# Forgetting attention: the key's forget sums and the causal mask added on VectorE instead of TensorE

## The chip, the cores and the metric

One core of a Trainium2 chip runs the whole program. The metric is the device time of one execution in microseconds, lower is better; the median of three runs of the kernel before is 2260.61 us (2258.91 to 2261.26).

## The reference, cut to what matters

Two layers on 512 tokens of width 2048. The second layer has three attention branches. Branch B, the one that is changed, is attention with forget gates: a running sum of log-gates per head is added to the scores.

```python
def forgetting_attention(q, k, v, f_logit, q_gain, k_gain):
    ...
    log_f = jax.nn.log_sigmoid(f_logit.astype(jnp.float32))
    c = jnp.cumsum(log_f, axis=1).transpose(0, 2, 1)
    ...
    def block_fn(args):
        qb, cqb, n = args
        sc = jnp.einsum('bqhd,bshd->bhqs', qb, k) * scale + cqb[..., None] - c[:, :, None, :]
        qpos = n * BLOCK + jnp.arange(BLOCK)
        mask = key_pos[None, :] <= qpos[:, None]
        sc = jnp.where(mask[None, None], sc, NEG)
        p = jax.nn.softmax(sc, axis=-1)
        return jnp.einsum('bhqs,bshd->bqhd', p, v)
```

B has 12 heads of 64 channels, 512 queries and 512 keys. The softmax of a row is the same without the query's own sum, which is one number for the whole row.

## The kernel before, in words

All matrix products use float32r operands. A float32 operand is split into a high part (a cast on ACT) and the rest (a subtraction on DVE), and a product becomes two or three products of parts. For weights, `Stream._piece` (L68) makes `whi` on ACT (L91) and `wlo` on DVE (L92) of each half of a tile that was loaded; it works two halves ahead of the products.

The program is written in the order in which the engines run it: each engine takes its instructions in program order. The main line is a sequence of projections (`proj`, L1236, or `logits`, L1288) into the PSUM banks `m0` to `m3`. Beside it, generators are advanced piece by piece: after each bank of a projection `step()` (L241) adds the generator's rate to a credit, and each full credit runs it to its next `yield`. The attention of a unit runs that way beside the projections of the next unit, at rate 0.41, one piece in about 2.4 steps, and what is left is run out by `drain()` ahead of the last tile of the second projection. There are six such units: one of kind C, two of A, three of B with four heads each. The three of B are called unit 0, 1 and 2 here; unit 2 runs beside the logits, whose results pass through `g` on DVE and ACT (L1295, L1296).

`attend` (L953) first normalizes and transposes queries and keys, whose splits go to `qk12` (L892 to L896). Then it goes through items. An item of B is a head and one of three sets of query blocks: blocks 0 and 1 with 128 and 256 keys, block 2 with 384, block 3 with 512. For each item there are these steps, of which two items are in flight:

- `s0` (L1049): score products into bank `s0` or `s1`, in turn; then on DVE the row maxima `nm` (L1084), and on ACT the exponentials into `pt`, with the sums of a row (L1089). In B each segment has two products `qk12` x key parts, one product that adds the key's sums (`cs`, a row selector scaled per head, times `mov`, the stored sums, L1067) and one that adds the mask to the diagonal block (`idr` x `dmr`, L1068). `cs` is made for the next head by ACT from `ct2` (L973, tile `cst`).
- `s2` (L1098), an iteration later: PE transposes the item's blocks of `pt` into the one bank `s2` (L1111), ACT casts them to `pth` (L1136) and DVE makes the rest, `ptl` (L1138), run by run.
- `s4` (L1140), when a head's last item is through: the products with the values into bank `s3`; `release` (L1019) then brings them to `os` (ACT L1029, DVE L1030), `finish` (L1032) divides by the row sums and gates with z (`un`), and `flush` (L1164) transposes that and writes `ur`.

`forget` (L907) makes the sums once, before the first unit: `mov` holds them for the products' moving side and `ct2` for the stationary side.

Kind A goes through the same steps. In its `s0` one DVE instruction adds a bias to the scores while it copies them to `pt` (L1080), and the maximum is taken from `pt` (L1082).

Of the kernel before, what the change touches and what calls it, by code (L numbers as in the profile page):

```python
# [14 lines left out]
P = 128  # L15
# [115 lines left out]
def _build(es, tc, nc, x, vecs, bgate, fg, sinks, bforget, w_mod, w_pin, w_grp, w_pout, mem, w_in, w_kv,  # L131
# [685 lines left out]
    idr = a3.tile([P, P], F32R, name="idr")  # L817
    S.copy(idr, idf)
    dmf = a3.tile([P, P], F32, name="dmf")
    nc.sync.dma_start(dmf, dmask)  # L820
    dmr = a3.tile([P, P], F32R, name="dmr")
    S.copy(dmr, dmf)
    rels = a3.tile([P, 256], F32, name="rels")
    nc.sync.dma_start(rels, rel)
    csl = a3.tile([P, 12], F32, name="csl")
    nc.sync.dma_start(csl, csel)
# [78 lines left out]
    ct2 = a3.tile([P, T], F32R, name="ct2")  # L905

    def forget(qk):  # L907
# [20 lines left out]
        for q in (32, 64, 96):  # L928
            V.tensor_copy(lf[:, :, q : q + 12], lf[:, :, 0:12])
# [7 lines left out]
        V.memset(r32(mov), 1.0)  # L937
        V.memset(r32(ct2), 1.0)
        S.copy(mov[0:64, :], b[0:64, :])
        V.tensor_tensor(out=mov[32:64, :], in0=b[32:64, :], in1=r32(mov[32:64, :]), op=sub)  # L940
        S.copy(ct2[64:128, :], b[64:128, :])
        V.tensor_tensor(out=ct2[96:128, :], in0=b[96:128, :], in1=r32(ct2[96:128, :]), op=sub)
# [10 lines left out]
    def attend(kind, unit, qk, vz):  # L953
# [12 lines left out]
        def head_state(h):  # L966
            if h not in hs:
                s = {}
                s["nm"] = a3.tile([P, NT], F32, tag="nm", name="nm", bufs=3)
                s["den"] = a3.tile([P, NT], F32, tag="den", name="den", bufs=3)  # L970
                if kind == "B" and "cs" not in s:
                    s["cs"] = a3.tile([P, T], F32R, tag="cst", name="cst", bufs=2)
                    S.activation(s["cs"], r32(ct2), AF.Copy, scale=csl[:, h0 + h : h0 + h + 1])  # L973
                hs[h] = s
            return hs[h]

        head_state(0)

# [70 lines left out]
        def s0(e):  # L1049
# [7 lines left out]
            for qt, c0, n in segs:  # L1057
                qs, bb = slice(qt * P, (qt + 1) * P), b[:, c0 : c0 + n]
                k0 = max(qt - 1, 0) * P if kind == "A" else 0
                ks = slice(k0, k0 + n)  # L1060
                if kind == "C":
                    mm3(bb, qkh[:, h, qs], qkl[:, h, qs], kch[:, h, ks], kcl[:, h, ks], True, True)
                else:
                    mm(bb, qk12[:, h, qs], kh[:, ks], start=True)
                    mm(bb, qk12[:, h, qs], kl[:, ks], stop=kind != "B")
                if kind == "B":
                    mm(bb, s["cs"][:, qs], mov[:, :n])  # L1067
                    mm(b[:, c0 + n - P : c0 + n], idr, dmr, stop=True)  # L1068
            if segs[0][0] == 0 and h + 1 < nh:
                head_state(h + 1)  # L1070
            pt = a3.tile([P, 512], F32, tag="pt", name="pt", bufs=2)
# [4 lines left out]
            for qt, m, c0, n in groups:  # L1076
                v = b[:, c0 : c0 + m * n].rearrange("p (m n) -> p m n", n=n)
                if kind == "A":
                    w = pt[:, c0 : c0 + m * n].rearrange("p (m n) -> p m n", n=n)
                    V.scalar_tensor_tensor(out=w, in0=rels[:, 256 - n :].unsqueeze(1).to_broadcast([P, m, n]), scalar=SLOPES[h0 + h],  # L1080
                                           in1=v, op0=mult, op1=add)
                    V.tensor_reduce(out=s["nm"][:, qt : qt + m], in_=w, axis=AX.X, op=vmax)  # L1082
                else:
                    V.tensor_reduce(out=s["nm"][:, qt : qt + m], in_=v, axis=AX.X, op=vmax, negate=True)  # L1084
# [3 lines left out]
            for qt, c0, n in segs:  # L1088
                S.activation(pt[:, c0 : c0 + n], (pt if kind == "A" else b)[:, c0 : c0 + n], AF.Exp, bias=s["nm"][:, qt : qt + 1],  # L1089
# [84 lines left out]

        ne = len(items)
        for e in range(ne + 2):
# [10 lines left out]
            if 1 <= e <= ne:  # L1187
                s2(e - 1)
            yield
# [177 lines left out]
def host_arrays(inputs):  # L1367
# [12 lines left out]
    for h in range(12):  # L1380
        csel[[h, 32 + h], h] = -1.0
        csel[[64 + h, 96 + h], h] = 1.0
# [31 lines left out]
```

## Time and profile before

| | |
|---|---|
| median of three runs | 2260.61 us |
| the profiled execution, its own time | 2261.89 us |
| its span, first to last instruction | 2260.1 us |
| mean granted TensorE clock | 0.993 of full speed |
| PE busy (matmuls) | 2212.2 us, 98% of the span |
| DVE busy | 1146.1 us, 51% |
| ACT busy | 883.1 us, 39% |
| attention of B, units 0, 1, 2 | begins about 1157, 1270 and 1385 us and lasts 60 to 70 us each |

PE is TensorE's matmuls, DVE VectorE, ACT ScalarE. Products go through the helper `mm` and so have the line L258 in every view. A row of the timeline gives an instruction's start and duration, its engine and line, and in square brackets how long the engine sat idle before it and what it then waited for last. Matmuls overlap in the pipeline, so what a product costs PE is the distance from its start to the next one's start, its pitch, and not its duration.

### The profile page before, as it was taken

Reading aid. Unit: us, or ns where it says so; the run is one execution under the profiler, and the core shown is the slowest. Engines: PE = TensorE matmul, PEld = TensorE weight load, DVE = VectorE, ACT = ScalarE, POOL = GpSimd, SP = SyncE. Lnnn points to the kernel's source line nnn. Section 1 sums busy time; section 2 is a strip of 40 time slices with the busy share of each in tenths; the row PEclk is TensorE's granted clock in tenths of the full one; section 3 lists DMA queues with packets and bytes.
Section 4 is the critical chain, followed back from the end, with each engine's and each line's share of the span. In section 5 each row is a group of like instructions: output and inputs, shape, how many; then the busy total and the mean of one; then the engine's idle time right before and its main releaser. Section 6 shows DMA issues by size and latency. Waiting matters only on the chain.

```text
span 2260.1 us, 26827 instructions
## 1 busy us (share of the span) xinstructions
PE 2212.2 (98%) x10199; PEld 1822.2 (81%) x10199; DVE 1146.1 (51%) x1996; ACT 883.1 (39%) x1719; POOL 0.2 (0%) x4
## 2 busy tenths in 40 slices
PE   7999999999999999999999999999999999999999
PEld 4678888888888988777778787788888888888887
DVE  3676655346665453756564655554334235336332
ACT  4433364333334353545464646542232222224221
POOL 0000000000000000000000000000000000000000
PEclk9989999999999999999999999999999999999999
DMA  9856633336664332222222222233333333333443
GB/s 329 280 165 208 202 103 98 98 121 225 223 224 128 97 83 75 75 75 75 75 75 75 75 75 75 66 100 96 94 93 102 97 99 94 102 94 98 154 131 112
DMA packets 164665, 275.12 MB, mean 122 GB/s; under 512 B 11074, under 2 KB 62776, under 8 KB 164280
## 3 DMA queue, kind: packets, MB, share of 16 engines
q1 hardware_dynamic: 164536, 273.41, 39.7%
q8 instruction: 80, 1.31, 0.2%
q14 instruction: 49, 0.40, 0.1%
HBM read 264.98 MB, written 8.39 MB: 121 GB/s over the span
## 4 chain that ended last, share of the span: by engine, by line
PE 82%; DVE 8%; ACT 5%; DMA 3%; issue 2%; SPq 0%; DVEq 0%; ACTq 0%
PE m L258 53%; PE s L258 26%; DVE wlo L92 2%; DVE qk L896 1%; DMA raw<-w_kv 1%; ACT pt L1089 1%; PE s L1111 1%; ACT whi L91 1%; DMA raw<-w_pout 1%; DVE acc L452 1%; ACT qk L892 1%; DVE nm L1082 1%; DVE pt L1080 1%; DVE ptl L1138 0%; DVE qk L862 0%
## 5 line engine op out<-in xcount | busy, mean ns | idle before, releaser
L92 DVE TENSOR_TENSOR wlo<-raw,whi 128x512 fp32r<-128x512 f32 (+2 forms) x740 | 493.7, 676 | 765.5 <-ACT whi L91 752.8
L91 ACT CAST whi<-raw 128x512 fp32r<-128x512 f32 (+2 forms) x740 | 441.3, 608 | 874.8 <-PE m L258 390.1
L258 PE MATMUL m<-whi,h_h 128*128 128x512 f32 (+2 forms) x960 | 373.8, 389 | 1.3 <-ACT whi L91 1.3
L258 PE MATMUL m<-wlo,h_h 128*128 128x512 f32 (+2 forms) x960 | 363.6, 379 | 2.9 <-DVE wlo L92 2.6
L258 PE MATMUL m<-whi,h_l 128*128 128x512 f32 (+2 forms) x960 | 363.1, 378 | 0.0
L258 PE MATMUL m<-h_h,whi 128*128 128x512 f32 x768 | 305.0, 397 | 0.0
L258 PE MATMUL m<-h_h,wlo 128*128 128x512 f32 x768 | 302.4, 394 | 1.0 <-DVE wlo L92 1.0
L258 PE MATMUL m<-h_l,whi 128*128 128x512 f32 x768 | 302.0, 393 | 0.0
L258 PEld LDWEIGHTS m<-wlo,h_h 128*128 128x128 f32 x960 | 181.5, 189 | 31.9 <-DVE wlo L92 6.1
L258 PEld LDWEIGHTS m<-whi,h_l 128*128 128x128 f32 x960 | 180.8, 188 | 31.5
L258 PEld LDWEIGHTS m<-whi,h_h 128*128 128x128 f32 x960 | 181.5, 189 | 27.6 <-ACT whi L91 1.6
L258 PE MATMUL s<-h_h,whi 128*128 128x512 f32 x512 | 200.8, 392 | 0.0
L258 PE MATMUL s<-h_l,whi 128*128 128x512 f32 x512 | 200.5, 392 | 0.0
L258 PE MATMUL s<-h_h,wlo 128*128 128x512 f32 x512 | 200.2, 391 | 0.0
L258 PEld LDWEIGHTS m<-h_h,wlo 128*128 128x128 f32 x768 | 145.7, 190 | 32.6 <-DVE wlo L92 1.5
L258 PEld LDWEIGHTS m<-h_h,whi 128*128 128x128 f32 x768 | 145.9, 190 | 30.4 <-ACT whi L91 0.8
L258 PEld LDWEIGHTS m<-h_l,whi 128*128 128x128 f32 x768 | 145.8, 190 | 29.6
L258 PEld LDWEIGHTS s<-h_h,wlo 128*128 128x128 f32 x512 | 96.8, 189 | 20.2
L258 PEld LDWEIGHTS s<-h_h,whi 128*128 128x128 f32 x512 | 96.8, 189 | 20.1
L258 PEld LDWEIGHTS s<-h_l,whi 128*128 128x128 f32 x512 | 96.9, 189 | 20.1
L258 PE MATMUL m<-whi,y_h 128*128 128x512 f32 x256 | 102.8, 402 | 1.4 <-DVE t L778 1.4
L258 PE MATMUL m<-whi,y_l 128*128 128x512 f32 x256 | 100.0, 391 | 0.0
(239 smaller groups left out, 2744.3 us busy)
## 6 DMA issues: line engine op xcount, KB each, us to landing
raw<-w_mod SPq DMA_DIRECT2D x96, 512.0 KB, 4.4
raw<-w_in SPq DMA_DIRECT2D x96, 512.0 KB, 3.8
raw<-w_pin SPq DMA_DIRECT2D x58, 512.0 KB, 3.8
raw<-w_in SPq DMA_DIRECT2D x96, 256.0 KB, 3.0
raw<-w_pout SPq DMA_DIRECT2D x32, 512.0 KB, 4.5
raw<-w_out SPq DMA_DIRECT2D x32, 512.0 KB, 3.7
raw<-w_in SPq DMA_DIRECT2D x32, 384.0 KB, 3.4
raw<-w_kv SPq DMA_DIRECT2D x16, 512.0 KB, 7.1
```

The costliest lines, as they stand in the source:

```text
L91: self.nc.scalar.copy(h3, v)
L92: self.nc.vector.tensor_tensor(out=l3, in0=v, in1=h3.bitcast(F32), op=ALU.subtract)
L258: PE.matmul(ps, lhsT=lhsT, rhs=rhs, start=start, stop=stop)
L452: V.scalar_tensor_tensor(out=acc, in0=v[:, e, :], scalar=w, in1=acc, op0=mult, op1=add)
L892: S.activation(hi[r, :], b[r, :], AF.Copy, scale=gain[r, :])
L896: V.scalar_tensor_tensor(out=outs[e][1][w, :], in0=b[r, :], scalar=gain[r, :], in1=r32(hi[r, :]), op0=mult, op1=sub)
L1080: V.scalar_tensor_tensor(out=w, in0=rels[:, 256 - n :].unsqueeze(1).to_broadcast([P, m, n]), scalar=SLOPES[h0 + h], in1=v, op0=mult, op1=add)
L1082: V.tensor_reduce(out=s["nm"][:, qt : qt + m], in_=w, axis=AX.X, op=vmax)
L1089: S.activation(pt[:, c0 : c0 + n], (pt if kind == "A" else b)[:, c0 : c0 + n], AF.Exp, bias=s["nm"][:, qt : qt + 1], accum_out=s["den"][:, ...
L1111: PE.transpose(b[:, x * P : (x + 1) * P], pt[:, c : c + P], idf)
```

## The change

In B's items the two products that add sums and mask are gone. PE leaves the scores in the bank; DVE adds the head's key sums while it moves them to `pt`, adds the mask to the diagonal block in `pt`, and takes the maximum from `pt`, as ACT takes the exponentials. The sums must now lie in every row, as `sums[h]` (tile `cst`, 128 x 512). `key_sums` makes them: one PE product of a selector `sel` with `mov` into bank `s3` and a copy by ACT. For a unit's first head it stands in a piece of its own ahead of the items, in bank `s0`; for the next head in the third item's iteration, behind `s2`. The selector (`pick`, 128 x 128) is made by ACT where `cs` was made. The queries' own sums are no longer added. The casts `idr` and `dmr`, `ct2`, two copies and a memset in `forget` are gone, and the rows of `csel` that served `ct2`.

```diff
-    idr = a3.tile([P, P], F32R, name="idr")
-    S.copy(idr, idf)
...
-    dmr = a3.tile([P, P], F32R, name="dmr")
-    S.copy(dmr, dmf)
...
-        for q in (32, 64, 96):
+        for q in (32,):
             V.tensor_copy(lf[:, :, q : q + 12], lf[:, :, 0:12])
...
-        V.memset(r32(mov), 1.0)
-        V.memset(r32(ct2), 1.0)
+        V.memset(r32(mov), 0.0)
         S.copy(mov[0:64, :], b[0:64, :])
         V.tensor_tensor(out=mov[32:64, :], in0=b[32:64, :], in1=r32(mov[32:64, :]), op=sub)
-        S.copy(ct2[64:128, :], b[64:128, :])
-        V.tensor_tensor(out=ct2[96:128, :], in0=b[96:128, :], in1=r32(ct2[96:128, :]), op=sub)
...
-                if kind == "B" and "cs" not in s:
-                    s["cs"] = a3.tile([P, T], F32R, tag="cst", name="cst", bufs=2)
-                    S.activation(s["cs"], r32(ct2), AF.Copy, scale=csl[:, h0 + h : h0 + h + 1])
...
+        def pick(h):
+            sel[h] = a3.tile([P, P], F32R, tag="sel", name="sel", bufs=2)
+            S.activation(sel[h], ones, AF.Copy, scale=ckl[:, h0 + h : h0 + h + 1])
+
+        def key_sums(h, tag="s3"):
+            b = bank(tag)
+            mm(b, sel.pop(h), mov, start=True, stop=True)
+            sums[h] = a3.tile([P, T], F32, tag="cst", name="cst", bufs=2)
+            S.copy(sums[h], b)
...
-                    mm(bb, qk12[:, h, qs], kl[:, ks], stop=kind != "B")
-                if kind == "B":
-                    mm(bb, s["cs"][:, qs], mov[:, :n])
-                    mm(b[:, c0 + n - P : c0 + n], idr, dmr, stop=True)
+                    mm(bb, qk12[:, h, qs], kl[:, ks], stop=True)
             if segs[0][0] == 0 and h + 1 < nh:
                 head_state(h + 1)
+                if kind == "B":
+                    pick(h + 1)
...
+                elif kind == "B":
+                    w = pt[:, c0 : c0 + m * n]
+                    V.tensor_tensor(out=w, in0=b[:, c0 : c0 + m * n], in1=sums[h][:, :n], op=add)
+                    dg = pt[:, c0 + n - P : c0 + n]
+                    V.tensor_tensor(out=dg, in0=dg, in1=dmf, op=add)
+                    V.tensor_reduce(out=s["nm"][:, qt : qt + m], in_=w, axis=AX.X, op=vmax, negate=True)
...
-                S.activation(pt[:, c0 : c0 + n], (pt if kind == "A" else b)[:, c0 : c0 + n], AF.Exp, bias=s["nm"][:, qt : qt + 1],
+                S.activation(pt[:, c0 : c0 + n], (b if kind == "C" else pt)[:, c0 : c0 + n], AF.Exp, bias=s["nm"][:, qt : qt + 1],
...
+        if kind == "B":
+            key_sums(0, "s0")
+            yield
         ne = len(items)
...
                 s2(e - 1)
+            if kind == "B" and e < ne and items[e][1][-1][0] == NT - 1 and items[e][0] + 1 < nh:
+                key_sums(items[e][0] + 1)
             yield
```

How the instructions stand now, at three places. The first is PE in unit 0 of B, the first item of the third head, before (`mov,cst` and `dmr,idr` are the products that go):

```order
L258 MATMUL s_9767<-qk_5578 128x128 x2
L258 MATMUL s_9767<-mov,cst 128x128
L258 MATMUL s_9767<-dmr,idr 128x128
L258 MATMUL s_9767<-qk_5578 128x256 x2
L258 MATMUL s_9767<-mov,cst 128x256
L258 MATMUL s_9767<-dmr,idr 128x128
L258 MATMUL m_9737<-whi,h_h_576 128x512
```

The same item on PE now, from the products of the projection ahead of it to those behind:

```order
L258 MATMUL m_9723<-whi,h_l_592 128x512
L258 MATMUL s_9785<-qk_5574 128x128 x2
L258 MATMUL s_9785<-qk_5574 128x256 x2
L258 MATMUL m_9724<-whi,h_h_576 128x512
L258 MATMUL m_9724<-wlo,h_h_576 128x512
```

Four products left this item, two each left the second and third. The second place is DVE from the third item of the second head to the first item of the third, in unit 0, before:

```order
L1030 TENSOR_TENSOR os<-s_9692,os 64x512
L1084 TENSOR_REDUCE nm<-s_9725 128x1
L1039 RECIPROCAL den<-den 128x4
L1043 TENSOR_TENSOR un<-vz,den 128x4x64
L92 TENSOR_TENSOR wlo<-raw,whi 128x512
L1138 TENSOR_TENSOR ptl<-s_9751,pth 128x128 x3
L1084 TENSOR_REDUCE nm<-s_9767 128x1 x2
```

And the same stretch of DVE now (`cst` holds the sums, `dmf` the mask):

```order
L1036 TENSOR_TENSOR os<-s_9701,os 64x512
L1090 TENSOR_TENSOR pt<-s_9738,cst 128x512
L1092 TENSOR_TENSOR pt<-pt,dmf 128x128
L1093 TENSOR_REDUCE nm<-pt 128x1
L1045 RECIPROCAL den<-den 128x4
L1049 TENSOR_TENSOR un<-vz,den 128x4x64
L1149 TENSOR_TENSOR ptl<-s_9755,pth 128x128 x3
L92 TENSOR_TENSOR wlo<-raw,whi 128x512
L1090 TENSOR_TENSOR pt<-s_9785,cst 128x128
```

Two adds stand ahead of each maximum, in the same place between the `ptl` of two items. The split `wlo` moved behind the `ptl`, since a piece more runs before the items and so each item meets the projection a few steps later; between a unit's first maximum or add and its last `ptl` there are 15 splits before and 15 now. The third place is the start of unit 0 on DVE, the last splits of queries and keys (`cols`) and the first item, before:

```order
L896 SCALAR_TENSOR_TENSOR qk_5578<-s_9465,cols,qk_5578 64x512 x2
L92 TENSOR_TENSOR wlo<-raw,whi 128x512
L896 SCALAR_TENSOR_TENSOR qk_5578<-s_9465,cols,qk_5578 64x512 x2
L1084 TENSOR_REDUCE nm<-s_9500 128x1 x2
L92 TENSOR_TENSOR wlo<-raw,whi 128x512
```

And now:

```order
L92 TENSOR_TENSOR wlo<-raw,whi 128x512
L892 SCALAR_TENSOR_TENSOR qk_5574<-s_9455,cols,qk_5574 64x512 x2
L92 TENSOR_TENSOR wlo<-raw,whi 128x512
L1090 TENSOR_TENSOR pt<-s_9507,cst 128x128
L1092 TENSOR_TENSOR pt<-pt,dmf 128x128
```

One weight split more stands ahead of the unit's first add. Unit 2 starts in the same way; in unit 1 a split stood there before, too.

## Rows read from the trace of the kernel before

**Rows 1.** The page's fourth part: shares of the chain of work that ended last, by engine.
```profile
PE 82%; DVE 8%; ACT 5%; DMA 3%; issue 2%; SPq 0%; DVEq 0%; ACTq 0%
```
**Rows 2.** Busy time by stretch, one row for each unit of B, from its first maximum to its last transposes: length, then busy us and instructions of PE, PE's weight loads, DVE, ACT and POOL, the granted TensorE clock, the DMA engines' share and GB/s.
```profile
1162.50:1220.00 57.50, 55.98 (x291) 46.84 (x290) 31.45 (x74) 30.60 (x85) 0.00 (x0) 1.00 0.24 70
1276.50:1335.50 59.00, 57.77 (x290) 48.41 (x291) 31.60 (x74) 30.72 (x85) 0.00 (x0) 0.97 0.24 72
1390.50:1452.50 62.00, 58.94 (x291) 47.97 (x291) 32.74 (x76) 37.04 (x91) 0.00 (x0) 0.97 0.22 65
```
**Rows 3.** Timeline of DVE, then of ACT, over a first item of a head in unit 1 (start us, duration us).
```profile
1304.08 0.61 DVE L1084 TENSOR_REDUCE nm<-s 128x1 f32<-128x128 f32 x2
1306.27 0.69 DVE L92 TENSOR_TENSOR wlo<-raw,whi 128x512 fp32r<-128x512 f32 x1 [1.57 <-ACT whi L91]
...
1308.74 0.69 DVE L92 TENSOR_TENSOR wlo<-raw,whi 128x512 fp32r<-128x512 f32 x1
1309.35 0.55 DVE L1084 TENSOR_REDUCE nm<-s 128x1 f32<-128x384 f32 x1
...
1303.74 0.73 ACT L973 ACTIVATE cst<-ct,csl 128x512 fp32r<-128x512 f32 x1
1304.81 0.37 ACT L1089 ACTIVATE pt<-s,nm 128x128 f32<-128x128 f32 x1 [0.34 <-DVE nm L1084]
...
1305.61 0.62 ACT L91 CAST whi<-raw 128x512 fp32r<-128x512 f32 x1
...
1309.99 0.58 ACT L1089 ACTIVATE pt<-s,nm 128x384 f32<-128x384 f32 x1 [1.28 <-DVE nm L1084]
```
**Rows 4.** Who waited for whom: us in total, times, longest us. First ACT, DVE and PE in the stretch of unit 0 (1162.5 to 1220), then ACT and DVE in that of unit 1 (1276.5 to 1335.5), then ACT in that of unit 2 (1390.5 to 1452.5).
```profile
ACT pt L1089 <- DVE nm L1084: 13.3, 11, 2.0
...
ACT pth L1136 <- PE s L1111: 4.0, 5, 1.8
...
DVE wlo L92 <- ACT whi L91: 10.6, 12, 2.8
...
PE s L1111 <- ACT pt L1089: 1.4, 1, 1.4
...
ACT pth L1136 <- PE s L1111: 3.9, 5, 1.7
...
DVE nm L1084 <- PE s L258: 0.5, 2, 0.4
...
ACT pth L1136 <- PE s L1111: 3.6, 4, 1.9
```
**Rows 5.** Timeline of unit 0: its first maxima, and the first cast of its last item.
```profile
1162.55 0.62 DVE L1084 TENSOR_REDUCE nm<-s 128x1 f32<-128x128 f32 x2
...
1219.63 0.27 ACT L1136 CAST pth<-s 128x128 fp32r<-128x128 f32 x1 [1.84 <-PE s L1111]
```
**Rows 6.** Timeline of PE: score products of a first item of B and the second and third product of the projection behind it; those of a second item of B and the second product behind it; those of a first item of A with the second product behind it (`m` is the projection's bank).
```profile
1302.46 0.34 PE L258 MATMUL s<-qk 128*128 128x128 f32 x2
...
1303.61 0.39 PE L258 MATMUL m<-wlo,h_h 128*128 128x512 f32 x1
1303.84 0.40 PE L258 MATMUL m<-whi,h_l 128*128 128x512 f32 x1
...
1307.28 0.51 PE L258 MATMUL s<-qk 128*128 128x384 f32 x2
...
1308.15 0.39 PE L258 MATMUL m<-wlo,h_h 128*128 128x512 f32 x1
...
956.11 0.62 PE L258 MATMUL s<-qk 128*128 128x128 f32 x4
...
956.79 0.40 PE L258 MATMUL m<-wlo,h_h 128*128 128x512 f32 x1
```
**Rows 7.** Timeline of DVE in two items of kind A, where an add (L1080) and a maximum (L1082) that needs it follow each other.
```profile
928.52 0.29 DVE L1080 SCALAR_TENSOR_TENSOR pt<-rels,s 128x128 f32<-128x128 f32 x1 [0.36 <-PE s L258]
928.84 0.29 DVE L1082 TENSOR_REDUCE nm<-pt 128x1 f32<-128x128 f32 x1
929.04 0.41 DVE L1080 SCALAR_TENSOR_TENSOR pt<-rels,s 128x256 f32<-128x256 f32 x1
929.49 0.42 DVE L1082 TENSOR_REDUCE nm<-pt 128x1 f32<-128x256 f32 x1
...
932.95 0.68 DVE L1080 SCALAR_TENSOR_TENSOR pt<-rels,s 128x512 f32<-128x512 f32 x1
933.66 0.69 DVE L1082 TENSOR_REDUCE nm<-pt 128x2 f32<-128x512 f32 x1
```
**Rows 8.** The group of ACT's copies out of bank `s3` over the whole span (busy us, mean ns; then idle time before them), and ACT's and DVE's timeline behind the last `pth` of a third item's step in unit 1.
```profile
L1029 ACT COPY os<-s 64x512 f32<-64x512 f32 x24 | 13.9, 581 | 9.7 <-PE s L258 9.2
...
1317.11 0.62 ACT L91 CAST whi<-raw 128x512 fp32r<-128x512 f32 x1
...
1317.77 0.69 DVE L92 TENSOR_TENSOR wlo<-raw,whi 128x512 fp32r<-128x512 f32 x1 [0.23 <-ACT whi L91]
```
**Rows 9.** Timeline of PE at the first transposes of unit 1, and two products of the projection behind them.
```profile
1279.05 1.14 PE L1111 MATMUL s<-idf,pt 128*128 128x128 f32 x3 [1.04 <-ACT pt L1089]
...
1280.85 0.63 PE L258 MATMUL m<-whi,h_l 128*128 128x512 f32 x1
1281.27 0.63 PE L258 MATMUL m<-whi,h_h 128*128 128x512 f32 x1
```

More of the change, by code (lines that the diff above doesn't have):

```diff
@@ L816, in _build @@
     a3 = p3.enter_context(tc.tile_pool(name="a3", bufs=1))
-    idr = a3.tile([P, P], F32R, name="idr")
-    S.copy(idr, idf)
     dmf = a3.tile([P, P], F32, name="dmf")
     nc.sync.dma_start(dmf, dmask)
-    dmr = a3.tile([P, P], F32R, name="dmr")
-    S.copy(dmr, dmf)
     rels = a3.tile([P, 256], F32, name="rels")
     nc.sync.dma_start(rels, rel)
-    csl = a3.tile([P, 12], F32, name="csl")
-    nc.sync.dma_start(csl, csel)
+    ckl = a3.tile([P, 12], F32, name="ckl")
+    nc.sync.dma_start(ckl, csel)
     snk = a3.tile([P, 12], F32, name="snk")
@@ L904, in _build @@
     mov = a3.tile([P, T], F32R, name="mov")
-    ct2 = a3.tile([P, T], F32R, name="ct2")
     def forget(qk):
@@ L970, in head_state @@
                 s["den"] = a3.tile([P, NT], F32, tag="den", name="den", bufs=3)
-                if kind == "B" and "cs" not in s:
-                    s["cs"] = a3.tile([P, T], F32R, tag="cst", name="cst", bufs=2)
-                    S.activation(s["cs"], r32(ct2), AF.Copy, scale=csl[:, h0 + h : h0 + h + 1])
                 hs[h] = s
             return hs[h]
+        sel, sums = {}, {}
+        def pick(h):
[6 more added lines that the diff above has]
+            S.copy(sums[h], b)
         head_state(0)
+        if kind == "B":
+            pick(0)
         if kind == "C":
@@ L1173, in flush @@
                 V.tensor_tensor(out=ur[chunk], in0=b, in1=os, op=mult)
+        if kind == "B":
+            key_sums(0, "s0")
+            yield
         ne = len(items)
@@ L1381, in host_arrays @@
         csel[[h, 32 + h], h] = -1.0
-        csel[[64 + h, 96 + h], h] = 1.0
     edge = np.ones((4, 2, 8), np.float32)
```

## The prediction, made before the changed kernel was run

> **What bounds the kernel now.** I read the page's chain first: 82% of the span lies on PE and 8% and 5% on DVE and ACT [rows 1]. So PE's own work sets the time, and a PE product that goes away is worth its pitch, as long as PE stays the last to be ready. The change takes products from PE and gives work to DVE in the forgetting attention (kind B), three units of four heads, three items a head. So the second view is the stretch of each unit, from the first `nm` of its first item to the last item's weights being split: there PE is busy 56 of 57.5, 57.8 of 59 and 58.9 of 62 us, DVE about 32 in each, ACT 31 to 37 [rows 2]. By those shares DVE has some 26 us a unit to spare.
>
> The third view, the timeline of DVE and ACT over one item, says otherwise. DVE takes the item's two maxima at 1304.08 and they end 0.61 us later; only then, at 1304.81, do ACT's exponentials begin; ACT's next weight copy `whi` comes behind them at 1305.61; DVE waits 1.57 us for it, splits `wlo` at 1306.27, then goes through three `ptl`, each behind an ACT `pth`; another `wlo` at 1308.74, and the next item's maximum at 1309.35, for which ACT in turn has waited 1.28 us until 1309.99 [rows 3]. Each engine's idle time is the other's work: the two form one serial chain of 5.3 us in that item. The waits say the same of a whole unit: in unit 0 ACT waits 13.3 us for DVE's maxima and DVE 10.6 us for `whi`, and the two wait for PE only where `pth` waits for the transposes: 4.0, 3.9 and 3.6 us in the three units, and 0.5 more where DVE waits for scores in unit 1 [rows 4]. So the pair has 4.0, 4.4 and 3.6 us of play in units of about 57 (1162.55 to 1219.63 [rows 5]), 59 and 62 us [rows 2]. PE's bound is real but thin: the pair is second, 7% behind.
>
> PE cannot run far ahead of the pair. An item's four transposes go to the one bank `s2`, which the `ptl` of the item before must have left, and they read `pt`, which the exponential must have written. A pair that is late holds PE at the transposes.
>
> **The change part by part.**
>
> *Products taken from PE.* A first item of B, from its first score product to the second projection product behind it, takes 1302.46 to 1303.61, 1.15 us; kind A's item with the same two segments and nothing added takes 956.11 to 956.79, 0.68 us [rows 6]. That is 0.47 saved. The second item takes 1307.28 to 1308.15, 0.87; a 512-column product follows the last at 0.23 (1303.61 to 1303.84), so two of 384 columns take 0.35 and with one projection product 0.58: 0.29 saved. The third, by the same steps with 512 columns, saves 0.23 for its key-sum product and 0.12 for the mask, 0.35. A head saves 1.11 and pays one `key_sums` product of 512 columns, 0.23. Net 0.88 a head, 10.6 us for 12, if PE stays the bound. The order shows that unit's pieces still end before the point where they would be drained, so the one piece more costs PE no drain.
>
> *Adds and masks put on DVE.* Between the score and the maximum there now stand an add from PSUM and a mask add in `pt`, each needing the one before. Kind A has the same dependent form: 128 columns to the next step 928.52 to 928.84, 0.32; 256 columns 929.04 to 929.49, 0.45; 512 columns 932.95 to 933.66, 0.71 [rows 7]. For 384 I take the middle of the last two, 0.58, and for a mask add the 0.32 of the same 128x128 size. First item: 0.32 + 0.32 + 0.45 + 0.32 = 1.41. Second: 0.58 + 0.32 = 0.90. Third: 0.71 + 0.32 = 1.03. A head gets 3.34 us, a unit 13.4. Nothing hides it: in that time ACT has nothing before the exponential that waits for it, which is what the 1.28 us before 1309.99 show [rows 3]. The first exponential of a first item waits for both maxima even now (1304.81 against 1304.08 + 0.61), so that item's four new instructions all count.
>
> *The sums' copy on ACT.* `key_sums` for the next head adds a copy of a bank, like `os` at 581 ns (L1029) [rows 8], behind the last `pth` of the third item's step. In the row of before `whi` follows that `pth` at once, at 1317.11, and `wlo` 0.66 later, at 1317.77, after waiting for it [rows 8]; the copy pushes both. I take 0.45 for three heads of a unit, 1.35. The old copy `cst` of 0.73 ran while ACT waited for the maxima (1303.74, before 1304.81 [rows 3]), so its going frees nothing on the chain; `sel`, a quarter of its size, goes to the same hole.
>
> *The start of a unit.* One piece more stands ahead of the first item. The order puts one more `wlo` ahead of the first add in units 0 and 2: its pitch is 0.61 (1308.74 to 1309.35 [rows 3]), so 0.6 there and nothing in unit 1, where one stands in that place already. The number of splits inside a unit stays 15.
>
> *What is dropped outside.* The casts of the identity and of the mask, `ct2` with its two steps, and two of three copies in `forget` lie long before the first unit, beside projection products that don't use them; I take them at nothing, and if uncovered they would be a gain of under 2 us. SP's queue keeps its DMAs.
>
> *The sum.* The pair's added time less the play it had: unit 0 13.4 + 1.35 + 0.6 - 4.0 = 11.3; unit 1 13.4 + 1.35 - 4.4 = 10.3; unit 2 13.4 + 1.35 + 0.6 - 3.6 = 11.7. Together 33.3 us. PE's saving is not subtracted: it only lengthens PE's waits at the transposes. The profiled execution takes 2261.89 us (its span 2260.1), so 2295.2; it lies 1.3 above the median of the three runs, hence 2294.
>
> *Bounds.* From below: only the four adds lie in series (0.32 + 0.45 + 0.58 + 0.71 = 2.06 a head, 8.2 a unit) and masks and copy are hidden; less the play that is 4.2 + 3.8 + 4.6 = 12.6, so 2274 and 2273 by the median. From above: PE's long waits lower its clock. After a wait of 1.04 us at 1279.05 its products follow at 0.42 (1280.85 to 1281.27) instead of 0.23 [rows 9], and the granted clock of units 1 and 2 is 0.97 [rows 2], part of it spent at 1.2 GHz instead of 2.4: of 59 us 0.03, 1.8 us lost, once in each. If nine more heads lose as much and none of it disappears in waits, 16 us come on top: 2310.
>
> **The rivals.**
>
> *PE stays the bound* (faster). The pair would take the new work into its idle time, PE keeps its saving, and the time is 2261.9 - 10.6 = 2251.3, 2250 by the median. For it: DVE is busy 31 to 33 of about 60 us [rows 2], and the chain lies on PE [rows 1]. Against it: the idle time is waiting for ACT [rows 3, 4]. The point from which it decides: the pair's added time must stay under its play, 4 us a unit or 1 us a head, while the bare four adds are 2.06. Chance 0.09. The Trainium skill leans this way: its page Perfetto Trace Analysis, section Identifying the Most-Contended Engine, calls the engine with the highest occupancy the one to work on first. By that rule PE should be relieved at DVE's cost and the time would fall as in this rival; the rows agree that PE's share is highest, but the waits show that shares don't tell how the other two depend on each other.
>
> *The two cancel.* If the pair's added time is just above its play, say 4 to 5 us a unit, the time stays within 4.5 us (0.2%, about what measurements of this kernel can tell from no change). It needs both masks and half the adds hidden. Chance 0.05.
>
> *The clock falls with the waits* (slower still). PE then works about 76% of a unit (56.0 less 4 x 0.88 saved, of 57.5 + 11.3 us); each head could lose 1.8 us as above. For it: both drops followed waits of a microsecond or more, like those to come. Against: PE waited 1.4 us in unit 0 [rows 4] and kept a granted clock of 1.00 [rows 2], and a slower PE mostly shortens its own waits, since the pair sets the pace. 2300 to 2310. Chance 0.12.
>
> *The pair takes the load and PE waits for it*, as summed: 2294. Chance 0.74.
>
> **How the numbers follow.** Slower has 0.74 + 0.12 = 0.86, no change 0.05, faster 0.09. The range runs from the lower bound, 2272, to the upper, 2311; it leaves out the two rivals that are not slower, 0.14, and little else.
>
> **What would show it.** In the changed profile the add of 128x512 should take near 0.7 us and a mask add near 0.3; a head should take about 18 us from its first add to the next head's, where it takes 57 / 4 = 14.3 now (14.3 less 1.0 of play, and 3.34 + 0.45 more, is 17.1; more where projections or logits leave their banks); PE should wait at the transposes for `ptl` or `pt` in most items, 10 us or more a unit, where it waited 1.4 in unit 0 [rows 4]; ACT's waits for `nm` should grow by about 3 us a head, and waits of `pth` for PE should nearly vanish. If PE has hardly any such waits and a unit is shorter than before, the chain of DVE and ACT was not serial and the forecast is wrong. If the granted clock of the units falls below 0.95, the third rival holds.

## The result, and the profile after

The changed kernel takes 2280.75 us (median of four runs, 2278.28 to 2281.34), the kernel before on the same chip 2260.94: 19.8 us slower, ratio 1.0078, interval 1.0066 to 1.0091. The forecast was 2294 in a range from 2272 to 2311. The sign and the mechanism held, the size was 13 us too large.

The chain of the page has moved towards VectorE, as DVE's share grew from 8% to 12% and PE's fell [rows 1]:

```profile
PE 75%; DVE 12%; ACT 7%; DMA 3%; issue 2%; SPq 0%; ACTq 0%; DVEq 0%
```

There is one trace of each kernel, and in the fourteen traces the first of the periods below begins anywhere from 1134.6 to 1141.4 us, though next to nothing ahead of it was changed. So kernels are compared here over the three units alone. The same four weight splits (numbers 361, 393, 425 and 457 of DVE's 740 `wlo`) bound three periods, each with the same projection work and one unit of B. Busy time of the three periods and their sum, before (columns as in [rows 2]):

```profile
1138.10:1250.60 112.50, 110.53 (x546) 91.70 (x545) 63.16 (x129) 61.15 (x136) 0.00 (x0) 1.00 0.26 75
1250.60:1366.10 115.50, 112.51 (x546) 93.13 (x545) 63.45 (x130) 61.36 (x136) 0.00 (x0) 0.99 0.25 73
1366.10:1479.90 113.80, 110.11 (x532) 90.45 (x531) 66.26 (x134) 66.45 (x141) 0.00 (x0) 0.99 0.25 73
sum 341.80, PE 333.15 PEld 275.28 DVE 192.88 ACT 188.96 POOL 0.00; mean PE 111.05 PEld 91.76 DVE 64.29 ACT 62.99 POOL 0.00
```

And after:

```profile
1138.20:1257.90 119.70, 110.99 (x517) 87.87 (x517) 75.52 (x161) 62.79 (x140) 0.00 (x0) 1.00 0.24 71
1257.90:1377.30 119.40, 110.25 (x517) 87.97 (x517) 75.56 (x161) 62.80 (x140) 0.00 (x0) 1.00 0.24 71
1377.30:1499.90 122.60, 111.81 (x509) 88.60 (x508) 78.39 (x165) 68.15 (x145) 0.00 (x0) 0.97 0.23 67
sum 361.70, PE 333.05 PEld 264.45 DVE 229.46 ACT 193.74 POOL 0.00; mean PE 111.02 PEld 88.15 DVE 76.49 ACT 64.58 POOL 0.00
```

The whole loss lies here: 361.7 - 341.8 = 19.9 us. Ahead of the first period the two kernels are equal (1138.1 and 1138.2), and behind the last period all fourteen traces agree within 1.6 us (779.4 to 781.0). DVE works 36.6 us longer, about what the forecast priced in its four adds and masks (3.34 x 12 = 40.1 us). PE's idle time (the length less PE's busy time) rose from 8.7 to 28.7 us, by the whole loss. Its busy time has not changed, though 28 products net went from each unit (8 a head, less one `key_sums` product a head; the rows count 29 in the first two, and some records of products can be missing); its weight loads are 10.8 us shorter. So PE's busy time doesn't tell how much work it has. Single products have not become longer (512 columns of `m` from `whi` and `h_h` took 413 ns in the mean before and 403 now); why the busy time stayed is not shown. The Trainium skill (Perfetto Trace Analysis, section Identifying the Most-Contended Engine) says that matmul busy time is no measure of PE's headroom and that weight loads are a better one. Here the trace agrees: PEld fell from 275.3 to 264.5 us as products went, 81% of the periods to 73%, while PE stayed at 333.

One first item of a head in unit 1, DVE and then ACT, answers to [rows 3]:

```profile
1314.65 0.29 DVE L1090 TENSOR_TENSOR pt<-s,cst 128x128 f32<-128x128 f32 x1 [0.20 <-ACT cst L979]
1314.98 0.29 DVE L1092 TENSOR_TENSOR pt<-pt,dmf 128x128 f32<-128x128 f32 x1
1315.31 0.29 DVE L1093 TENSOR_REDUCE nm<-pt 128x1 f32<-128x128 f32 x1
1315.51 0.41 DVE L1090 TENSOR_TENSOR pt<-s,cst 128x256 f32<-128x256 f32 x1
1315.96 0.29 DVE L1092 TENSOR_TENSOR pt<-pt,dmf 128x128 f32<-128x128 f32 x1
1316.29 0.42 DVE L1093 TENSOR_REDUCE nm<-pt 128x1 f32<-128x256 f32 x1
1317.88 0.69 DVE L92 TENSOR_TENSOR wlo<-raw,whi 128x512 fp32r<-128x512 f32 x1 [1.18 <-ACT whi L91]
...
1315.69 0.40 ACT L1100 ACTIVATE pt<-pt,nm 128x128 f32<-128x128 f32 x1 [0.77 <-DVE nm L1093]
...
1316.74 0.51 ACT L1100 ACTIVATE pt<-pt,nm 128x256 f32<-128x256 f32 x1 [0.55 <-DVE nm L1093]
...
1317.25 0.60 ACT L91 CAST whi<-raw 128x512 fp32r<-128x512 f32 x1
```

Each step starts where the one before it lets it: 0.33 and 0.45 us for add, 0.33 for mask, as priced. From the item's first DVE step to `whi` it is 2.60 us, where it was 1.53 (1304.08 to 1305.61 [rows 3]): 1.07 of the 1.41 put in; ACT now waits between its two exponentials as well, since the second maximum comes late for it. Unit 0's waits of ACT (1163.4 to 1231) show the same against [rows 4]:

```profile
ACT pt L1100 <- DVE nm L1093: 23.6, 16, 2.7
...
ACT pth L1147 <- PE s L1122: 0.6, 1, 0.6
```

ACT's wait for maxima grew by 10.3 us, 2.6 a head; its wait for PE has nearly gone (4.0 to 0.6): the pair's play is used up. PE's own waits, over all three periods:

```profile
PE s L1122 <- DVE ptl L1149: 8.4, 6, 2.1
PE s L258 <- ACT cst L979: 6.0, 3, 2.1
PE s L258 <- DVE os L1036: 4.9, 6, 0.9
PE s L258 <- DVE ur L1184: 4.2, 3, 1.6
PE s L258 <- DVE ptl L1149: 2.0, 3, 0.9
PE s L258 <- ACT pth L1147: 1.9, 2, 1.7
```

Only 8.4 us lie at the transposes. 6.0 are of a new kind: at each unit's start the first scores wait for the sums' copy to leave bank `s0`. In the 4.9 and 4.2, products wait for `os` to leave `s3` and for `flush` to leave a score bank. That list suggests another cause than the forecast's: banks. Whether these waits make the loss or only show it was the first thing to test.

### The profile page after: what moved, and what is told of

The parts are those of the page before. It is cut to its first block, busy times and chain, and to the rows that moved or that the text cites. A ratio compares the mean times of both kernels' runs of the same rounds, so it can differ in the third digit from the quotient of the medians.

```text
span 2279.4 us, 26749 instructions
## 1 busy us (share of the span) xinstructions
PE 2211.3 (97%) x10115; PEld 1809.9 (79%) x10115; DVE 1181.9 (52%) x2088; ACT 887.1 (39%) x1728; POOL 0.2 (0%) x4
## 4 chain that ended last, share of the span: by engine, by line
PE 75%; DVE 12%; ACT 7%; DMA 3%; issue 2%; SPq 0%; ACTq 0%; DVEq 0%
PE m L258 49%; PE s L258 25%; DVE wlo L92 3%; ACT whi L91 2%; ACT pt L1100 1%; DVE ptl L1149 1%; DVE qk L892 1%; DMA raw<-w_kv 1%; DVE nm L1093 1%; DVE pt L1090 1%; DMA raw<-w_pout 1%; ACT pth L1147 1%; DVE pt L1092 1%; ACT qk L888 1%; DVE nm L1087 1%
```

## The experiments

"Three periods" is the sum of the same three stretches, 341.8 us before and 361.7 in the changed kernel; the ratio is that of run times to the kernel before. Each sum comes from one trace. The ratios, taken of 2261 us, give the sums' differences to the kernel before within 3.2 us in every row but one (free banks, 5.1), so rows that lie closer than that are not told apart here.

| run | ratio (95% interval) | three periods |
|---|---|---|
| the change | 1.0078 (1.0066 to 1.0091) | 361.7 |
| VectorE's half alone | 1.0105 (1.0085 to 1.0125) | 366.3 |
| TensorE's half alone | 0.9965 (0.9951 to 0.9979) | 336.4 |
| no mask adds | 1.0023 (1.0013 to 1.0032) | 348.8 |
| free banks | 1.0066 (1.0051 to 1.0081) | 361.8 |
| no piece | 1.0115 (1.0098 to 1.0132) | 368.2 |
| before, with a piece | 0.9974 (0.9964 to 0.9985) | 336.3 |
| TensorE's saving given back | 1.0088 (1.0069 to 1.0106) | 364.0 |
| pieces at 0.8, items at 0.31 | 1.0146 (1.0129 to 1.0163) | 374.6 |
| items at 0.36 | 1.0070 (1.0052 to 1.0087) | 357.9 |
| one head's sums for all | 1.0066 (1.0051 to 1.0081) | 359.9 |
| mask on TensorE, items at 0.36 | 1.0010 (1.0000 to 1.0021) | 345.9 |
| before, with a piece, items at 0.36 | 1.0001 (0.9992 to 1.0011) | 342.4 |

**VectorE's half alone.** In the kernel before:

```diff
+                elif kind == "B":
+                    w = pt[:, c0 : c0 + m * n]
+                    V.tensor_tensor(out=w, in0=b[:, c0 : c0 + m * n], in1=r32(ct2[:, :n]), op=add)
+                    dg = pt[:, c0 + n - P : c0 + n]
+                    V.tensor_tensor(out=dg, in0=dg, in1=dmf, op=add)
+                    V.tensor_reduce(out=s["nm"][:, qt : qt + m], in_=w, axis=AX.X, op=vmax, negate=True)
...
-                S.activation(pt[:, c0 : c0 + n], (pt if kind == "A" else b)[:, c0 : c0 + n], AF.Exp, bias=s["nm"][:, qt : qt + 1],
+                S.activation(pt[:, c0 : c0 + n], (b if kind == "C" else pt)[:, c0 : c0 + n], AF.Exp, bias=s["nm"][:, qt : qt + 1],
```

> The kernel before with VectorE's half of the change alone: the products that add sums and mask stay on TensorE, and VectorE does an add of the same size and a mask add of the same size in front of each maximum (the added tile is the stored sums of ct2 and the mask a second time, so the scores of B are not the reference's). No sums' copy, no extra piece, no product fewer. Theory, the pair of ScalarE and VectorE is one serial chain that sets B's pace: TensorE's products then lie inside its waits, so keeping them costs nearly nothing; four adds and four masks, 3.34 us a head, less 4 us of play a unit, +9 us a unit or less, 2276 to 2288, close to the changed kernel's 2281. Rival, the two effects add up, TensorE's saving of 10.6 us being real in the changed kernel: 2281 + 10.6 = 2291 or more. Rival, the new waits for banks make the loss: this kernel has none of them, so it gives back 12 us and lies at 2269 or below.

2287.12 us; its three periods:

```profile
sum 366.30, PE 339.92 PEld 274.97 DVE 229.67 ACT 191.72 POOL 0.00; mean PE 113.31 PEld 91.66 DVE 76.56 ACT 63.91 POOL 0.00
```

24.5 us more than before without any of the change's new waits for banks: that rival falls. It is inside the first theory's range, but not close to the changed kernel's 2281: it lies 6 us above it, more than half of the way to the second line's 2291. What those 6 us are is settled only by the runs on the piece and on TensorE's saving below.

**TensorE's half alone.** In the changed kernel the branch `elif kind == "B"` with its adds and both calls of `key_sums` go, and the exponential reads the bank in B:

```diff
-                elif kind == "B":
-                    w = pt[:, c0 : c0 + m * n]
...
-            key_sums(0, "s0")
-            yield
...
-                key_sums(items[e][0] + 1)
```

> TensorE's half of the change alone: the products that add sums and mask are gone, and so are the adds on VectorE, the sums' product, its copy and its piece; maximum and exponential read the bank as before. B's sums and causal mask are left out. Theory (TensorE was the bound in the kernel before, with 4 us of play to the pair in each unit): TensorE saves 4 x 1.11 = 4.4 us a unit, 13.3 in all, and the pair's play covers most of it: 2247 to 2253. If the pair were already the bound: 2257 to 2261. If the full saving needs no play: 2247.

2253.54 us, half a us above the first range. In the periods:

```profile
sum 336.40, PE 321.63 PEld 262.83 DVE 192.59 ACT 184.68 POOL 0.00; mean PE 107.21 PEld 87.61 DVE 64.20 ACT 61.56 POOL 0.00
```

PE is busy 11.5 us less, the periods fall by 5.4 (the runs by 0.35%, 7.9 us, with an interval from 4.7 to 11.1): even with no load added to DVE, a part of PE's saving is lost.

**No mask adds.** Two lines of the changed kernel go:

```diff
-                    dg = pt[:, c0 + n - P : c0 + n]
-                    V.tensor_tensor(out=dg, in0=dg, in1=dmf, op=add)
```

> The changed kernel without the four mask adds of a head (the causal mask of B is left out); everything else stays, the sums' adds and both new waits for banks included. Theory of the serial pair: each mask add is 0.32 us in the chain, 1.28 a head, 5.1 a unit, 15.4 in all; the time falls by 10 to 15 us to 2266 to 2271. Rival, waits for banks (s0 at a unit's start, s3 at the next head's sums) make the loss: they stay, and the time falls by under 5 us, to 2276 or more.

2266.30 us, in the first range. The periods fall by 12.9 us for 13.7 us of DVE:

```profile
sum 348.80, PE 330.19 PEld 266.51 DVE 215.78 ACT 193.59 POOL 0.00; mean PE 110.06 PEld 88.84 DVE 71.93 ACT 64.53 POOL 0.00
```

A DVE instruction in this chain costs nearly its full time, on an engine that is idle for over a third of the stretch.

**Free banks.**

```diff
-            key_sums(0, "s0")
+            key_sums(0, "s1")
...
-            if kind == "B" and e < ne and items[e][1][-1][0] == NT - 1 and items[e][0] + 1 < nh:
+            if kind == "B" and e < ne and items[e][1][0][0] == 0 and items[e][0] + 1 < nh:
```

> The changed kernel with the sums' product in places where its bank is free: the first head's in bank s1 instead of s0, which the first item's scores take next, and a next head's two items earlier, when s3 has long been left by os. In the trace of the changed kernel TensorE waits 2.0 us for the copy out of s0 at each unit's start and about 0.9 us for os before two of three sums' products, 3.9 us a unit, 11.7 in all. Rival, these waits are the loss: the time falls by 9 to 12 us to 2269 to 2272. Theory of the serial pair: VectorE and ScalarE start no earlier and go no faster, TensorE waits as long at its next meeting with them, and the time stays within 4 us, 2277 to 2282.

2277.01 us, in the ratio 0.12% (2.7 us) under the change, with intervals that overlap. The trace is 3.5 us shorter than the change's, all of it ahead of the first period, and the periods are the same 361.8. PE's waits over the three periods now read:

```profile
PE s L1122 <- DVE ptl L1149: 11.4, 10, 2.4
PE s L258 <- ACT cst L979: 10.7, 6, 3.0
...
PE s L258 <- DVE qk L892: 3.6, 3, 1.2
```

The waits for `os` are gone, and so are those of the first scores for the copy; in their place the value products wait for the early copy to leave `s3` (all six times), the sums' product waits 1.2 us at each unit's start for DVE's `qk`, and the transposes wait longer. So the banks did not become free, the waits moved: PE meets the pair somewhere, at whatever bank comes first. That the waits for banks show the loss and don't make it rests on this run together with VectorE's half alone, which has no `key_sums` and the full loss.

**No piece.** The changed kernel without the `yield` behind the first head's sums:

```diff
-            key_sums(0, "s0")
-            yield
+            key_sums(0, "s1")
```

> The changed kernel without the piece of its own for the first head's sums: the product stands in the same piece as the first item's scores (and in bank s1, so that those scores don't wait for the copy). The items then meet the projection where they met it in the kernel before, 9 projection products (2.0 us) earlier than in the changed kernel. The prediction held that the piece costs 0.6 us in two units. Theory now: VectorE is late at a unit's start with the splits of queries and keys, as in the kernel before, where the first maximum came 5.4 us after the first scores; the extra piece gives it 2 us of projection to catch up. So without it each unit loses 1.5 to 2 us: 4 to 6 us more than the variant with free banks and the piece (2277), 2281 to 2284. By the prediction's step: 1 us less, 2276.

2288.03 us, and in the periods 6.4 more than with piece and free banks, more than expected. Two things differ between those two runs, the piece and where the later heads' sums are made; against the change itself, where the sums of later heads stand alike and the first head's bank differs, it is 6.5. By unit it is 1.6, 4.3 and 0.6 us more than in the change:

```profile
1137.20:1258.50 121.30, 112.07 (x517) 89.01 (x516) 75.62 (x161) 62.83 (x140) 0.00 (x0) 0.99 0.24 70
1258.50:1382.20 123.70, 112.35 (x518) 88.98 (x517) 75.69 (x162) 62.82 (x140) 0.00 (x0) 0.99 0.24 68
1382.20:1505.40 123.20, 111.27 (x506) 88.23 (x505) 78.66 (x166) 68.42 (x145) 0.00 (x0) 0.97 0.23 67
```

**Before, with a piece.**

```diff
+        if kind == "B":
+            yield
         ne = len(items)
```

> The kernel before with one empty piece ahead of the items of each unit of B, nothing else: its items come 9 projection products later, as in the changed kernel. Theory that the start of a unit is where VectorE is late: TensorE's waits at the first transposes (1.4 us in unit 0, 0.9 + 1.0 in unit 1, 0.7 in unit 2, and the half clock for 3.4 us behind that of unit 1, 1.6 us lost) go: 3 to 6 us less, 2256 to 2259 where the kernel before has 2262. If the piece is worth nothing, or costs a weight split: 2261 to 2264.

2257.06 us, ratio 0.9974: an empty piece makes the kernel before faster, by 5.5 us in the periods; by unit 1.3, 4.3 and nothing (0.1 us more):

```profile
1139.80:1251.00 111.20, 110.65 (x546) 91.55 (x545) 63.35 (x130) 61.12 (x136) 0.00 (x0) 1.00 0.26 77
1251.00:1362.20 111.20, 110.61 (x546) 91.51 (x545) 63.24 (x129) 61.15 (x136) 0.00 (x0) 1.00 0.26 76
1362.20:1476.10 113.90, 111.17 (x536) 91.05 (x535) 66.16 (x133) 66.40 (x141) 0.00 (x0) 0.99 0.25 73
```

This is the fastest kernel here that leaves nothing of the computation out.

**TensorE's saving given back.** In the changed kernel:

```diff
-                    mm(bb, qk12[:, h, qs], kl[:, ks], stop=True)
+                    mm(bb, qk12[:, h, qs], kl[:, ks], stop=kind != "B")
+                    if kind == "B":
+                        mm(bb, qk12[:, h, qs], kl[:, ks])
+                        mm(b[:, c0 + n - P : c0 + n], qk12[:, h, qs], kl[:, (qt * P) : (qt + 1) * P], stop=True)
```

> The changed kernel with TensorE's saving given back: each segment gets two more products of the sizes of those that went (the low part of the keys once more over all keys and once more over the diagonal block, so B's scores are off by that small part). 0.47 + 0.29 + 0.35 = 1.11 us of TensorE a head, 13.3 us for the 12. Theory of the serial pair, as in the prediction: these products lie in TensorE's waits, 2280 to 2284. Rival, TensorE's saving counts in full beside the pair: 2281 + 13 = 2294. Rival, VectorE's add comes right behind the scores' last product in some items and is delayed by those alone: 2284 to 2288.

2281.62 us, beside 2280.75: 13.3 us of products cost 2.3 in the periods and cannot be told from nothing in the runs. PE's idle time falls from 28.7 to 20.6 us, so most of them lie in PE's waits:

```profile
sum 364.00, PE 343.39 PEld 279.20 DVE 229.88 ACT 193.56 POOL 0.00; mean PE 114.46 PEld 93.07 DVE 76.63 ACT 64.52 POOL 0.00
```

**Another pace.** In the changed kernel the rate becomes a variable, set where a unit begins and where its items begin:

```diff
-                credit[lane] += side[0][1]
+                credit[lane] += side[0][1][0] if isinstance(side[0][1], list) else side[0][1]
...
+        pace[0] = 0.8 if kind == "B" else 0.41
...
+        pace[0] = 0.31 if kind == "B" else 0.41
         items = [(h, segs) for h in range(nh) for segs in parts]
...
-        aside(attend(kind, unit, qk2, vz2), 0.41)
+        aside(attend(kind, unit, qk2, vz2), pace)
```

> The changed kernel with the same pieces at another pace: B's pieces ahead of the items (norms, transposes, splits) at rate 0.8 instead of 0.41, and those of the items at 0.31, so that 18 to 21 projection products lie between two items' transposes instead of 12 to 15, and a unit's items end where they ended. Theory of the serial pair: it needs 17 to 18 us a head, with a half split more for the longer stretch; TensorE then brings 10.2 x 19.5 / 15 + 3.7 = 17 us of work a head instead of 13.9, and its waits of 12 us a unit shrink to 1 to 5: 2281 less 20 to 30, 2252 to 2263, if the faster pieces ahead cost nothing. Rival, VectorE's added work costs its time wherever it stands: 2276 or more. Rival, the faster pieces ahead of the items make TensorE wait there instead: 2265 to 2275.

2295.16 us: a miss, slower than any. PE's waits over the three periods:

```profile
PE s L884 <- DVE qk L858: 16.0, 5, 5.9
PE s L258 <- ACT cst L982: 14.2, 3, 5.0
```

They lie ahead of the items (transposes of queries and keys) and at the first scores; at the items' transposes there are none. But six of these waits, of 4.3 to 5.9 us, each came with a fall of the granted clock to half, and the three periods have 0.93, 0.95 and 0.94, the first of them:

```profile
1141.40:1268.10 126.70, 112.35 (x510) 91.41 (x510) 76.19 (x162) 62.22 (x138) 0.00 (x0) 0.93 0.23 67
```

By these figures (0.07 x 126.7 + 0.05 x 124.1 + 0.06 x 123.8) some 22 us of full clock are missing, part of them while PE waited anyway; in the change it is 0.03 x 122.6 = 4. The run is 12.9 us slower than the change, so it doesn't tell what the pace is worth. The next run left the pieces ahead at 0.41:

```diff
+        pace[0] = 0.41 if kind == "B" else 0.41
...
+        pace[0] = 0.36 if kind == "B" else 0.41
```

> The changed kernel with the pieces ahead of the items at 0.41 as before and those of the items at 0.36, so that 15 to 18 projection products lie between two items' transposes (12 to 15 in the changed kernel) and a unit's last transposes come 24 products, 5.4 us, later. The last experiment mixed two things: its items met no waits at the transposes, but the faster pieces ahead of them made TensorE wait 5 us twice a unit. Theory of the serial pair: with the pieces ahead left alone, TensorE's waits inside the items fall by up to 5.4 us a unit, 16 in all: 2265 to 2272. Rival, VectorE's added work costs its time at any pace: 2278 or more.

2276.66 us, 3.8 less in the periods than the change: neither range. The waits at the items fell (`ptl` 8.4 to 4.4, `os` 4.9 to 0.7), but where the projection runs out what is left of the unit, PE now waits for results to leave their banks behind those pieces:

```profile
PE m L258 <- DVE g L1315: 4.2, 1, 4.2
PE m L258 <- DVE qk L838: 3.3, 2, 1.7
PE m L258 <- ACT qk L836: 1.9, 2, 1.4
```

The same pace in the kernel before with the piece has its price alone:

> The kernel before with the empty piece ahead of the items (2257 with that alone) and B's items at 0.36. Theory of the serial pair: in that kernel TensorE hardly waits any more (0.6, 0.6 and 2.7 us in the three units' periods), so that the pace can give 0 to 2 us: 2255 to 2258. A rival by which a slower pace is a gain of its own, whoever is late: 2245 to 2250.

2263.22 us, 342.4 against 336.3 in the periods, against both lines: 0.7, 1.4 and 4.0 us lost by unit, with `m` waiting for `g` and `qk` at their end. If the price of 6 us is the same in the changed kernel, which no run shows, 0.36 frees about 10 us there and pays 6. With the mask as TensorE's product as well (and its two casts made again):

```diff
-                    mm(bb, qk12[:, h, qs], kl[:, ks], stop=True)
+                    mm(bb, qk12[:, h, qs], kl[:, ks], stop=kind != "B")
+                if kind == "B":
+                    mm(b[:, c0 + n - P : c0 + n], idr, dmr, stop=True)
...
-                    V.tensor_tensor(out=dg, in0=dg, in1=dmf, op=add)
```

> The changed kernel with the mask back on TensorE as a product into the bank (identity x mask, as before the change), the sums' adds left on VectorE, and the items at 0.36. Without mask adds the chain was 14.5 us shorter (2266); the masks' products cost TensorE about 0.1 us each, 0.3 to 0.5 a head, 4 to 6 us if they counted. Theory of the serial pair: TensorE's waits left inside the items (5 to 8 us a unit) go for the most part: 2252 to 2259, near or below the kernel before (2262). If the pace is worth nothing: 2266 to 2270.

2265.15 us, above the first range. In the periods 345.9 is 2.9 under the run without any mask: the mask's products are covered, and what the pace gives is too little to be told from nothing. No form of the change tried here that computes the whole reaches the kernel before with the piece.

**One head's sums for all four.** `pick` and `key_sums` of the next heads go:

```diff
-                if kind == "B":
-                    pick(h + 1)
...
-                    V.tensor_tensor(out=w, in0=b[:, c0 : c0 + m * n], in1=sums[h][:, :n], op=add)
+                    V.tensor_tensor(out=w, in0=b[:, c0 : c0 + m * n], in1=sums[0][:, :n], op=add)
...
-            if kind == "B" and e < ne and items[e][1][-1][0] == NT - 1 and items[e][0] + 1 < nh:
-                key_sums(items[e][0] + 1)
```

> The changed kernel with the sums of a unit's first head used for all four: the next heads' product in s3, its copy by ScalarE and their selectors are left out, so B's sums are wrong for three heads of four; adds and masks stay. The prediction put the copies at 0.45 us x 3 heads, 1.35 a unit, 4.05 in all. If they lie in the chain as put: 2281 - 4 = 2277. If VectorE hides them behind its wlo and adds: 2280 to 2282. If TensorE's waits for os before these products count too: 2281 - 4 - 5.6 = 2271.

2277.15 us, but only 1.8 us less than the change in the periods, between the first two lines; as much again lies ahead of them. By unit it is 1.3 and 1.1 us less and, in unit 2, 0.6 more (123.2 us, at a granted clock of 0.96 where the change has 0.97):

```profile
sum 359.90, PE 333.08 PEld 266.01 DVE 229.04 ACT 186.64 POOL 0.00; mean PE 111.03 PEld 88.67 DVE 76.35 ACT 62.21 POOL 0.00
```

## Why the prediction was right, and where its size came from

| term of the sum | forecast | measured | from |
|---|---|---|---|
| DVE's adds and masks (3 x 13.4), less the pair's play | 40.2 - 12.0 = 28.2 | 24.5 | VectorE's half alone |
| the sums' copies | 4.05 | 1.8 | one head's sums |
| the start of the units (two splits of 0.6) | +1.2 | -6.4 | no piece against free banks |
| TensorE's saving | 0 | 0 to -2.3 | saving given back |
| sum | 33.3 | 18 to 20 | the change: 19.9 |

- **The bound.** Shown. Four runs say that the pair sets the pace: DVE's half alone has the loss (8.1, 8.3 and 8.1 us by unit), DVE's masks cost 94% of their time, 13 us of PE are nearly free, and other banks change nothing in the periods. The rule of the Trainium skill that the prediction cites (Perfetto Trace Analysis, section Identifying the Most-Contended Engine), to work on the engine with the highest occupancy first, would have led the wrong way here, since it speaks for the change: PE relieved by 11.5 us of busy time gave 5.4, DVE loaded with 36.8 cost 24.5.
- **DVE's work less the play.** Right in its method, 3.7 us too large, little more than single traces tell. The forecast charged each first item of a unit in full; that one case went another way. Before, ACT's table load for the first exponential waited for the maxima, then the exponential for the load. ACT from the first maximum at 1162.55 [rows 5]:

```profile
1163.25 1.28 ACT L1089 ACT_TABLE_LOAD   x1 [1.52 <-DVE nm L1084]
1164.55 0.37 ACT L1089 ACTIVATE pt<-s,nm 128x128 f32<-128x128 f32 x1
...
1165.35 0.62 ACT L91 CAST whi<-raw 128x512 fp32r<-128x512 f32 x1
```

  Now the load runs ahead of them, beside DVE (the first row is DVE's):

```profile
1163.42 0.29 DVE L1090 TENSOR_TENSOR pt<-s,cst 128x128 f32<-128x128 f32 x1
...
1162.68 1.28 ACT L1100 ACT_TABLE_LOAD   x1
1164.40 0.40 ACT L1100 ACTIVATE pt<-pt,nm 128x128 f32<-128x128 f32 x1 [0.43 <-DVE nm L1093]
...
1166.01 0.60 ACT L91 CAST whi<-raw 128x512 fp32r<-128x512 f32 x1
```

  From DVE's first step to `whi` it was 2.80 us and is 2.59, though four instructions were put in. Before, the exponential waited for two engines, PE's bank and DVE's maximum, and the wait for DVE stood at the load ahead of it; now it reads `pt` and waits for DVE alone, at itself. Charged with 1.41 a unit, it gave 0.2: 1.6 x 3 = 4.9 us, enough for the 3.7. It reads the same in all three units and in VectorE's half alone; it was read from the traces, not tested by itself. Nor does the account close: the first item of a later head above gave 0.3 of its 1.41 back as well, which for the other nine would be 3 us more.
- **The step that failed: the start of a unit.** The prediction priced the extra piece at a `wlo`, 0.6 us in two units, 1.2 us of loss. It gains 6.4. The order had shown that each item "meets the projection a few steps later", and the step didn't price that. The piece puts 9 projection products, 2 us, ahead of each item. DVE, which comes to a unit's first item 5.4 us behind the first scores of PE (1157.15 in the trace before, against 1162.55 [rows 5]), uses them to catch up: it reaches the first item 25.2 us into the period instead of 24.5, while PE reaches each of its meetings with the pair 2 us later in its own work. With the empty piece in the kernel before DVE is only 4.0 us behind. PE's first scores of unit 0 before, then PE's and DVE's first step with the piece:

```profile
1157.15 0.34 PE L258 MATMUL s<-qk 128*128 128x128 f32 x2
...
1161.03 0.34 PE L258 MATMUL s<-qk 128*128 128x128 f32 x2
...
1164.98 0.62 DVE L1084 TENSOR_REDUCE nm<-s 128x1 f32<-128x128 f32 x2
```

  The two pairs of runs with and without the piece, in the kernel before and in the changed one, give 5.5 and 6.4 us. That the piece gains is shown; that it gains alike in each unit is not: in both kernels most of it falls in unit 1 (4.3 us) and next to nothing in unit 2, where before and with the piece PE waits about 2 us for `ptl` later on (1.67 at 1415.09, 2.00 at 1412.93). In unit 1 of the kernel before the piece also spares the stretch at half clock of [rows 9].
- **The sums' copy.** 1.8 of 4.05, a difference that single traces don't tell. In units 0 and 1 the copies gave 1.3 and 1.1 us, near the 1.35 priced, in unit 2 nothing. Whether a part of them is hidden stays open.
- **TensorE's saving.** Right: not on the path, or for 2.3 us at most.
- **What would show it.** A head takes 18.2 and 17.3 us behind the first head of unit 0 (first adds at 1163.42, 1177.10, 1195.26, 1212.56), as forecast, but 13.7 in the first. PE's waits at the transposes were forecast at 10 us a unit and are 1.4 in unit 0: PE's idle time is about as long as thought, 28.7 us in the three periods, but most of it lies at other banks. The order of PE's program should have told where it meets the pair first. (An item has three transposes, the third item of a head four, and not four in each.)
- **The rival with the clock** fell. The granted clock of the periods is 1.00, 1.00 and 0.97 after, 1.00, 0.99 and 0.99 before: 0.03 x 122.6 less 0.01 x 115.5 and 0.01 x 113.8 is 1.4 us more lost, not 16, and that is within the rounding of these figures: either trace has two short stretches at half clock in its periods. The rival is not wrong in kind, as the run with pieces at 0.8 shows, with its waits of 4.3 to 5.9 us and a clock of 0.93 to 0.95; the change's waits are of 2.1 us at most.

## What to carry to other kernels

An engine that is half idle may still be full, if its idle time is another engine's work: add the series of both over one round of the loop, subtract the time in which they wait for a third, and price an added instruction at its full length beyond that. Waits of PE for banks are then a symptom; test that by freeing the bank before believing it. And where work is fed to engines piece by piece, look at the phase: one empty piece at the right place took 5.5 us off the kernel before, as much as taking 11.5 us of TensorE's busy time away did (5.4).

## What the runs showed of the hardware that was not expected

PE's busy time stayed at 333 us of three periods with 10.8 us less of weight loads and 19.9 us more of span; its idle time grew by as much as the span. A table load of 1.28 us on ACT either ran ahead of the exponential's wait for DVE or stood behind it: before, ACT sat idle 1.52 us for DVE and then loaded, now it loads first, with no idle time in front, and waits 0.43 us for DVE behind the load. And PE waited 2.0 us at 1161.77 and 1.6 at 1215.24 in a period with a granted clock of 1.00, where in the kernel before a wait of 1.04 us was followed by products at half pace [rows 9].
